# Strassen's seven half products in place of eight in a SwiGLU feed-forward on one Trainium2 core

## The chip, the core and the metric

The kernel runs on one core of one Trainium2 chip, in one launch. The metric is the device time of one execution in microseconds. Engines are named as in the profile: PE is TensorE (matmuls), PEld its weight loads, DVE the vector engine, ACT the scalar engine, POOL the GpSimd engine, SP the engine whose queue issues the DMAs. SBUF is the on-chip working memory, PSUM the eight banks of 512 fp32 columns into which matmuls accumulate.

## What is computed

One layer of a hybrid diffusion backbone on 128 context tokens and 512 latent tokens of width 1024: a modulated RMSNorm, one input projection, a bidirectional gated DeltaNet beside a Conformer branch, a gated merge and an output projection, and then the feed-forward, which alone the change touches. Cut to that (FF_DIM is 2816):

```python
h2 = rmsnorm(x, norm2) * (1 + sc2) + sh2
gu = h2 @ w_gu                                   # (640, 1024) @ (1024, 2 * 2816)
x = x + g2 * ((jax.nn.silu(gu[..., :FF_DIM]) * gu[..., FF_DIM:]) @ w_down)
y = rmsnorm(x, norm_f)
```

All inputs and outputs are fp32.

## The kernel before

The 640 tokens are five tiles of 128. Activations that feed a projection stand transposed: 128 channels on the partitions, tokens along the columns. Each fp32 operand of a large matmul is split into a high part (ACT copies it to the rounded type fp32r) and a low part (`split`, L106 to L108: the difference, on DVE or POOL), and each product is three matmuls: high x high, high x low, low x high, all accumulating in one bank.

The feed-forward goes by column tiles of 128 of the 2816 gate and up columns, 22 in all. For a tile, `load_w` (L117) loads two weight blocks (gate and up), each 1024 channels x 128 columns laid out as 8 k tiles, into one of four raw slots ("wr", cycled by `w_next`); the high part goes into one of two "wh" buffers, the low part takes the raw slot's place ("wl"; here POOL makes it). `proj` (L131) runs 8 k tiles x 3 terms x 2 column groups (256 and 384 tokens) for each of the two. ACT applies Silu to gate from PSUM (L1252), DVE multiplies by up from PSUM (L1254), and the product "ft" is split into "fh" and "fl".

The tiles go in three parts of 8, 8 and 6. After each part, `tok_proj` multiplies the part's tiles by their rows of w_down, for each of two halves of 512 output columns: the blocks of two k tiles go one after the other over the five token tiles, and the last `tail` blocks are left to a loop over token tiles that ends each tile's sum and calls `done`. There `residual` (L1129, L1130) multiplies the sum by the gate row and adds it to x1. In the last part `done` goes on with the sum of squares (L1134, L1137), a power on POOL (L153), the products with norm_f (L1204, L1209) and with the row scale (L1211 to L1215), and the output DMA. The last half of the last part keeps all of its three w_down blocks (`load_end`).

The first two tiles are run in two steps, first over the two token tiles that are ready (their 256-column group), while the norm of the others (`after_wo`, which writes h2h and h2l) is still under way. Engines work their queues in order. The order is made when the program is built: a list scheduler takes the instructions by priority (the order of the program, but for the scans of the DeltaNet, which come first) and by when their inputs and buffers are ready in its own timeline. Buffers of a tag ("wh", "sub", "C", "H") are given out when an instruction is scheduled; the "wr" slots and, after the change, "v2" and "F" are bound when the program is written.

Of the kernel before, what the change touches and what calls it, by code (L numbers as in the profile page):

```python
# [9 lines left out]
F32 = mybir.dt.float32  # L10
# [46 lines left out]
def hybrid_step(ctx, tc, I, O):  # L57
# [5 lines left out]
    base = -(-nc.sbuf_base // 32) * 32  # L63
    nc.alloc_sbuf_tensor("weights", [P, 1024 * NWR], F32)
    w_slots = [(nc.alloc_sbuf_tensor_at(f"wr{i}", [P, 1024], F32, offset=base + 4096 * i).ap(),
# [9 lines left out]

    BUFS = {"wh": NWH, "sub": 3, "H": 4, "K": 4, "Q": 3, "C": 4, "F": 2, "dd": 3, "v2": 3, "S": 1}
    SIZE = {"wh": 1024, "sub": 1024, "H": 4 * COLS, "K": CONV + 3 * COLS,
            "Q": 4 * COLS, "C": CONV + 4, "F": COLS, "dd": 256, "v2": 512, "S": 512}

    def T_(tag, name, dt=F32, cols=None):  # L80
        return sb.tile([P, cols or SIZE[tag]], dt, tag=tag, name=name, bufs=BUFS[tag])

# [17 lines left out]
    def g3(ap, a):  # L100
        return ap.rearrange("p (a b) -> p a b", a=a)
# [26 lines left out]
    def cols_of(w, c0, n=P):  # L128
        return w[:, c0:c0 + n].rearrange("(k p) c -> p k c", p=P)
# [937 lines left out]

    def s2_tile(name):
        return s2p.tile([P, 1024], F32R, tag="w2", name=name, bufs=6)

# [126 lines left out]
    def after_down(n, last):
        def done(i, pt):
# [19 lines left out]

    def load_end(src, lo_eng=None):
        wh = s2_tile("wh2")  # L1220
        wr, wl = next(w_next)
        nc.sync.dma_start(out=g3(wr, 2), in_=src)
        split(wh, wl, wr, V)
        return g3(wh, 2), g3(wl, 2)

    f0 = 0
    for part, nf in enumerate((8, 8, 6)):
        fh = [g3(T_("H", f"fh{q}", F32R), 4) for q in range(2)]
        fl = [g3(T_("H", f"fl{q}", F32R), 4) for q in range(2)]
        for f in range(nf):  # L1230
            if f0 + f == 0:

                cut, early2 = HALVES, []
                for k in range(2):
                    w2 = w_first if k == 0 else [load_w(cols_of(wgu, FF * j + 128), lo_eng=(V, G)[j],
                                                        wh=s2_tile("wh2")) for j in range(2)]
                    early2.append((w2, mm_pair()))
                    for w, pb in zip(*early2[k]):
                        proj(w, h2h, h2l, NK, (pb, None), (0,), cut, True)
            if f0 + f < 2:  # L1240
# [12 lines left out]
            for s, d in halves(pup, t, cut):
# [34 lines left out]
```

## Time and profile before

| | us |
|---|---|
| median of 3 runs | 1339.76 (1338.90 to 1341.18) |
| the profiled execution, its own time | 1341.02 |
| its span, first to last instruction | 1339.2 |

The profile is of one execution. Times in its rows are microseconds from the start of the span, except where a mean duration stands in nanoseconds. A matmul's duration includes its pipeline; the pace of a stretch is its length divided by its matmuls. An idle time is put down to the instruction that came last of those that were waited for.

### The profile page before, as it was taken

The page shows a single profiled execution, that of the slowest core. Times are in us where ns is not written, and L with a number is a line of the kernel's source. Part 1 is how long each engine was busy: PE and PEld are TensorE (multiplying, and loading weights), DVE is VectorE, ACT ScalarE, POOL GpSimd, SP SyncE. Part 2 cuts the span into 40 slices and gives each one's busy share as a digit, 9 for nine tenths or more (in the row PEclk, how much of TensorE's full clock was granted, in tenths as well). Part 3 has the DMA queues.
Part 4 walks back from the last instruction along what each step waited for, and adds up shares of the span by engine and source line. Part 5 has one row for each costly group of instructions (what it writes and reads, how often), then busy time and mean ns, then how long its engine had stood idle before and what let it go on. Part 6 is the DMA issues. An engine that isn't in the chain of part 4 may idle for free.

```text
span 1339.2 us, 23242 instructions
## 1 busy us (share of the span) xinstructions
PE 1278.0 (95%) x9180; PEld 1203.7 (90%) x9180; DVE 845.0 (63%) x1663; ACT 505.2 (38%) x1080; POOL 299.7 (22%) x306
## 2 busy tenths in 40 slices
PE   4998998997999999999998999999999999999997
PEld 4998997997998999999988998899988999889996
DVE  5788996989667899998687774621224212243136
ACT  3426646254354554525354323422221222112223
POOL 2103312220110312211010036433300333003304
PEclk8998999999999999999999999999999999999999
DMA  9523353343343453324456882122222222222222
GB/s 290 153 64 97 113 167 123 112 139 99 109 122 102 142 144 101 105 78 128 142 188 202 286 281 87 52 76 79 79 74 70 78 80 75 68 79 79 79 68 91
DMA packets 180333, 157.31 MB, mean 117 GB/s; under 512 B 9072, under 2 KB 151809, under 8 KB 180225
## 3 DMA queue, kind: packets, MB, share of 16 engines
q1 hardware_dynamic: 180225, 155.83, 37.6%
q8 instruction: 72, 1.18, 0.4%
q14 instruction: 36, 0.29, 0.1%
HBM read 131.80 MB, written 24.00 MB: 116 GB/s over the span
## 4 chain that ended last, share of the span: by engine, by line
PE 57%; DVE 8%; DMA 3%; issue 2%; ACT 2%; POOL 1%; SPq 0%; POOLq 0%; DVEq 0%; ACTq 0%
PE mm L143 36%; PE sm L1108 9%; PE mm L1108 4%; PE sm L143 1%; DVE wl L108 1%; PE sm L729 1%; DVE uacc L843 1%; PE sm L753 1%; PE sm L656 1%; DVE uacc L840 1%; PE sm L1153 1%; PE sm L716 1%; PE sm L709 1%; PE sm L739 1%; DMA wr<-in_w_in 1%
## 5 line engine op out<-in xcount | busy, mean ns | idle before, releaser
L107 ACT ACTIVATE wh<-wr 128x1024 fp32r<-128x1024 f32 (+1 forms) x154 | 152.6, 992 | 477.2 <-PE mm L143 186.1
L143 PE MATMUL mm<-hh,wh 128*128 128x256 f32 (+1 forms) x896 | 217.6, 318 | 0.9 <-ACT wh L107 0.9
L143 PE MATMUL mm<-hl,wh 128*128 128x256 f32 (+1 forms) x896 | 215.4, 314 | 0.0
L108 POOL TENSOR_TENSOR wl<-wr,wh 128x1024 fp32r<-128x1024 f32 (+1 forms) x59 | 133.2, 2259 | 356.7 <-ACT wh L107 337.2
L143 PE MATMUL mm<-hh,wl 128*128 128x256 f32 (+1 forms) x896 | 212.5, 314 | 0.0
L108 DVE TENSOR_TENSOR wl<-wr,wh 128x1024 fp32r<-128x1024 f32 (+1 forms) x95 | 109.7, 1155 | 105.7 <-ACT wh L107 94.4
L143 PEld LDWEIGHTS mm<-hh,wh 128*128 128x128 f32 x896 | 161.5, 190 | 6.8 <-issue 4.6
L143 PEld LDWEIGHTS mm<-hl,wh 128*128 128x128 f32 x896 | 164.5, 189 | 0.0
L143 PEld LDWEIGHTS mm<-hh,wl 128*128 128x128 f32 x896 | 162.7, 189 | 0.3 <-issue 0.2
L143 PE MATMUL mm<-h2h,wh 128*128 128x256 f32 (+1 forms) x672 | 155.7, 309 | 0.0
L143 PE MATMUL mm<-h2l,wh 128*128 128x256 f32 (+1 forms) x672 | 154.9, 308 | 0.0
L143 PE MATMUL mm<-h2h,wl 128*128 128x256 f32 (+1 forms) x672 | 154.6, 307 | 0.0
L1254 DVE TENSOR_TENSOR ft<-ft,mm 128x256 f32<-128x256 f32 (+1 forms) x42 | 18.6, 481 | 189.9 <-PE mm L143 189.8
L143 PEld LDWEIGHTS mm<-h2l,wh 128*128 128x128 f32 x672 | 123.1, 188 | 0.0
L143 PEld LDWEIGHTS mm<-h2h,wl 128*128 128x128 f32 x672 | 122.7, 188 | 0.0
L143 PEld LDWEIGHTS mm<-h2h,wh 128*128 128x128 f32 x672 | 122.0, 188 | 0.2
L478 DVE SCALAR_TENSOR_TENSOR acc<-ci,colA,acc 128x642 f32<-128x642 f32 x96 | 85.8, 894 | 7.6 <-ACT acc L476 7.1
L1108 PE MATMUL sm<-wh,fl 128*128 128x512 f32 x152 | 60.0, 395 | 0.0
L1108 PE MATMUL sm<-wh,fh 128*128 128x512 f32 x152 | 59.8, 393 | 0.0
L1108 PE MATMUL sm<-wl,fh 128*128 128x512 f32 x152 | 59.6, 392 | 0.0
L108 DVE TENSOR_TENSOR fl<-ft,fh 128x640 fp32r<-128x640 f32 x22 | 46.5, 2112 | 16.5 <-ACT fh L107 16.5
L604 DVE TENSOR_TENSOR stmp<-M,X 128x30 f32<-128x30 f32 (+14 forms) x120 | 44.6, 372 | 2.6 <-POOL X L598 1.0
(347 smaller groups left out, 2446.8 us busy)
## 6 DMA issues: line engine op xcount, KB each, us to landing
wr<-in_w_in SPq DMA_DIRECT2D x56, 512.0 KB
wr<-in_w_gu SPq DMA_DIRECT2D x44, 512.0 KB
wr<-in_w_ada SPq DMA_DIRECT2D x32, 512.0 KB
wr<-in_w_down SPq DMA_DIRECT2D x22, 512.0 KB
wada<-in_w_ada SPq DMA_DIRECT2D x8, 1024.0 KB
atd<-et SPq DMA_DIRECT2D x40, 128.0 KB
aux<-atd SPq DMA_DIRECT2D x40, 128.0 KB
tgd<-tgt SPq DMA_DIRECT2D x16, 320.0 KB
```

The source lines that it names most:

```text
L107: S_.activation(hi, x, AF.Identity)
L108: return (lo_eng or V).tensor_tensor(out=lo, in0=x, in1=hi.bitcast(F32), op=ALU.subtract)
L143: PE.matmul(out, a[:, kt, :], x, start=(kt == 0 and j == 0), stop=(kt == nk - 1 and j == 2))
L478: V.scalar_tensor_tensor(out=acc[:, :n], in0=ci[:, k:k + n], scalar=vA[:, k, ct:ct + 1], in1=acc[:, :n], op0=ALU.mult, op1=ALU.add)
L604: V.tensor_tensor(out=t, in0=bc(M[:, j + 1:, j:j + 1], [P, n, j]), in1=bc(X[:, j:j + 1, 0:j], [P, n, j]), op=ALU.mult)
L656: PE.matmul(pt[:, j, :], lhs[j], rhs[j], start=True, stop=True)
L709: PE.matmul(pr[:, d, j, :], TT[j].kT[:, ck[d], :], S[:, d, j, :], start=True, stop=True)
L716: PE.matmul(pq[:, d, j, :], TT[j].q2[:, OFFC[ck[d]]:OFFC[ck[d]] + P], S[:, d, j, :], start=True, stop=True)
L729: PE.matmul(pv[:, d, j, :], Y1[:, d, j, ck[d], :], rhs, start=True, stop=True)
L739: PE.matmul(pS[:, d, j, :], TT[j].ktok[:, ck[d], :], vw[:, d, j, :], start=True, stop=True)
L1108: PE.matmul(acc[i], a[kt // 4][:, kt % 4, c], b[:, k2, :], start=(kt == 0 and j == 0), stop=(kt == nk - 1 and j == 2))
L1254: V.tensor_tensor(out=d, in0=d, in1=s, op=ALU.mult)
```

## The change

For 19 of the 22 column tiles (all but the first three), gate and up, split into channel halves, form a 2 x 2 block matrix (a11, a12: gate, first and second 512 channels; a21, a22: up), and the transposed activations one of channel halves by token halves (b11 to b22, 64 of each token tile's 128 tokens: 320 columns). Eight half products become seven, in a variant of Strassen's scheme that shares its sums.

- `gate_up`, per tile: loads the same two blocks; DVE makes four sums of 512 columns; seven 512-column operands are split (ACT the high part, POOL the low); seven products of 4 k tiles x 3 terms with 320 columns; ACT copies the first from PSUM, DVE adds seven times from PSUM, ACT makes two Silus, DVE two products into ft, and ft is split as before.
- `sums`, once: four sums of activation blocks, each from high and low parts, and their splits: per k tile of a half ten DVE sums and four splits of 320 columns, with the low parts on DVE.
- The parts are 3, 4, 4, 4, 3 and 4 tiles, with one set of fh and fl of 4 tiles; down has 24 blocks in place of 22, and 60 residuals in place of 30.
- `load_end` goes; the last half has `tail` 2 of its 2 blocks and uses load_w.
- Buffers: "v2" (3 of 512 columns) and "F" (2 of 640) become fixed blocks, given out in turn; the four sums of a tile take four of these five. The seven high parts take four buffers out of the cycle wh, sub, sub, wh, sub, w2. The half products' banks are given out as sm, ma, sm, mb, which are all eight. norm_f's row moves to two other places, in two DMAs.

```diff
     base = -(-nc.sbuf_base // 32) * 32
-    nc.alloc_sbuf_tensor("weights", [P, 1024 * NWR], F32)
+
+    fixed = {"v2": (3, 512), "F": (2, COLS)}
+    nc.alloc_sbuf_tensor("weights", [P, 1024 * NWR + sum(n * c for n, c in fixed.values())], F32)
+    homes, at = {}, base + 4096 * NWR
+    for tag, (n, c) in fixed.items():
+        homes[tag] = []
+        for i in range(n):
+            homes[tag].append({dt: nc.alloc_sbuf_tensor_at(f"{tag}{i}{nm}", [P, c], dt, offset=at).ap()
+                               for dt, nm in ((F32, "f"), (F32R, "r"))})
+            at += 4 * c
+        homes[tag] = cycle(homes[tag])
...
-    BUFS = {"wh": NWH, "sub": 3, "H": 4, "K": 4, "Q": 3, "C": 4, "F": 2, "dd": 3, "v2": 3, "S": 1}
+    BUFS = {"wh": NWH, "sub": 3, "H": 4, "K": 4, "Q": 3, "C": 4, "dd": 3, "S": 1}
...
     def T_(tag, name, dt=F32, cols=None):
+        if tag in homes:
+            return next(homes[tag])[dt]
         return sb.tile([P, cols or SIZE[tag]], dt, tag=tag, name=name, bufs=BUFS[tag])
...
-    def s2_tile(name):
-        return s2p.tile([P, 1024], F32R, tag="w2", name=name, bufs=6)
+    def s2_tile(name, tag="w2", cols=1024):
+        return s2p.tile([P, cols], F32R, tag=tag, name=name, bufs=2 if tag == "T" else 1)
...
-        wh = s2_tile("wh2")
+        if q % 2 == 0:
+            whole.append(s2_tile("wh2", "T", 4 * COLS))
+        wh = whole[-1][:, 1024 * (q % 2):1024 * (q % 2) + 1024]
...
-            wr, wl = T_("sub", "wr2"), s2_tile("wl2")
+            wr, wl = T_("sub", "wr2"), T_("sub", "wl2", F32R) if q == 2 else s2_tile("wl2")
...
-    g2b = T_("Q", "g2b")[:, :2 * D].rearrange("p (r c) -> p r c", r=2)
+    g2t = T_("Q", "g2b")
+    g2b = g2t[:, :2 * D].rearrange("p (r c) -> p r c", r=2)
     for r in range(2):
         nc.sync.dma_start(out=g2b[:, r, :], in_=gdr[1, r].partition_broadcast(P))
-    nfb = T_("sub", "nfb")
-    nc.sync.dma_start(out=nfb, in_=I["norm_f"].partition_broadcast(P))
+    nfb = [g2t[:, 2 * D:], T_("S", "nfb")]
+    for n in range(2):
+        nc.sync.dma_start(out=nfb[n], in_=I["norm_f"][512 * n:512 * n + 512].partition_broadcast(P))
...
-    def load_end(src, lo_eng=None):
...
+    HT = 64
+    T4 = NCH * 4 * HT
+    fh = [g3(T_("H", "fh", F32R), 4)]
+    fl = [g3(T_("H", "fl", F32R), 4)]
+
+    def sums():
+
+        both = [T_("H", "tb", F32R) for _ in range(2)] + [s2_tile("tb", "T", 4 * COLS) for _ in range(2)]
+        hi = [t[:, :T4].rearrange("p (i k c) -> p i k c", k=4, c=HT) for t in both]
+        lo = [t[:, T4:2 * T4].rearrange("p (i k c) -> p i k c", k=4, c=HT) for t in both]
+        for k in range(4):
+            ta, tb = T_("C", "t12")[:, :COLS], T_("C", "t34")[:, :COLS]
+            f = [g3(t[:, c:c + NCH * HT], NCH) for t in (ta, tb) for c in (0, NCH * HT)]
+            (b11, b12), (b21, b22) = ([[t[:, :, k, HT * b:HT * b + HT].bitcast(F32) for t in (h2h[q], h2l[q])]
+                                       for b in range(2)] for q in range(2))
+
+            def op(n, a, b, o):
+                V.tensor_tensor(out=f[n], in0=a, in1=b, op=o)
+            op(0, b12[0], b11[0], ALU.subtract)
+            op(0, f[0], b12[1], ALU.add)
+            op(0, f[0], b11[1], ALU.subtract)
+            op(1, b22[0], f[0], ALU.subtract)
+            op(1, f[1], b22[1], ALU.add)
+            op(2, b22[0], b12[0], ALU.subtract)
+            op(2, f[2], b22[1], ALU.add)
+            op(2, f[2], b12[1], ALU.subtract)
+            op(3, b21[0], f[1], ALU.subtract)
+            op(3, f[3], b21[1], ALU.add)
+            for n in range(4):
+                split(hi[n][:, :, k], lo[n][:, :, k], f[n])
+        return list(zip(hi, lo))
+
+    hi_tag, sum_tag = cycle(("wh", "sub", "sub", "wh", "sub", "w2")), cycle(("v2", "F", "v2", "F", "v2"))
+    bank_tag = cycle(("sm", "ma", "sm", "mb"))
+
+    def gate_up(f, k):
+        raw = []
+        for j in range(2):
+            wr, wl = next(w_next)
+            nc.sync.dma_start(out=g3(wr, NK), in_=cols_of(wgu, FF * j + 128 * f))
+            raw += [(wr[:, c:c + 512], wl[:, c:c + 512]) for c in (0, 512)]
+        a11, a12, a21, a22 = raw
+        sm = []
+        for _ in range(4):
+            home = next(homes[next(sum_tag)])
+            sm.append((home[F32][:, :512], home[F32R][:, :512]))
+        for k_, (a, b, o) in enumerate(((a21, a22, ALU.add), (None, a11, ALU.subtract), (a11, a21, ALU.subtract),
+                                        (a12, None, ALU.subtract))):
+            x = (a or sm[0])[0]
+            y = (b or sm[1])[0]
+            V.tensor_tensor(out=sm[k_][0], in0=x, in1=y, op=o)
+        ops = []
+        for n, (x, lo) in enumerate((a11, sm[1], a12, sm[2], sm[0], a22, sm[3])):
+            if n % 2 == 0:
+                tag = next(hi_tag)
+                hi2 = s2_tile("wh") if tag == "w2" else T_(tag, "wh", F32R)
+            hi = hi2[:, 512 * (n % 2):512 * (n % 2) + 512]
+            split(hi, lo, x, G)
+            ops.append((g3(hi, 4), g3(lo, 4)))
+        b11, b21, b22 = ((h2h[q][:, :, :, HT * b:HT * b + HT], h2l[q][:, :, :, HT * b:HT * b + HT])
+                         for q, b in ((0, 0), (1, 0), (1, 1)))
+        t1, t2, t3, t4 = tsum
+        right = (b11, t2, b21, t3, t1, t4, b22)
+
+        def product(n):
+            (wh, wl), (xh, xl) = ops[n], right[n]
+            tag = next(bank_tag)
+            bank = ps.tile([P, 512], F32, tag=tag, name="mm", bufs=4 if tag == "sm" else 2)[:, :NCH * HT]
+            for kt in range(4):
+                for j, (a, b) in enumerate(((wh, xh), (wh, xl), (wl, xh))):
+                    PE.matmul(g3(bank, NCH), a[:, kt, :], b[:, :, kt, :], start=(kt == 0 and j == 0),
+                              stop=(kt == 3 and j == 2))
+            return bank
+
+        def add(out, a, pt):
+            V.tensor_tensor(out=out, in0=a, in1=pt, op=ALU.add)
+        N2 = NCH * HT
+        ca, cb = T_("C", "ca"), T_("C", "cb")
+        c11, c12, c21, c22 = ca[:, :N2], ca[:, N2:2 * N2], cb[:, :N2], cb[:, N2:2 * N2]
+        t = T_("C", "ft")[:, :COLS]
+        tv = t.rearrange("p (i c) -> p i c", c=2 * HT)
+        S_.activation(c11, product(0), AF.Identity)
+        add(c12, c11, product(1))
+        add(c11, c11, product(2))
+        S_.activation(c11, c11, AF.Silu)
+        add(c21, c12, product(3))
+        p5 = product(4)
+        add(c22, c21, p5)
+        add(c12, c12, p5)
+        add(c21, c21, product(5))
+        V.tensor_tensor(out=tv[:, :, :HT], in0=g3(c11, NCH), in1=g3(c21, NCH), op=ALU.mult)
+        add(c12, c12, product(6))
+        S_.activation(c12, c12, AF.Silu)
+        V.tensor_tensor(out=tv[:, :, HT:], in0=g3(c12, NCH), in1=g3(c22, NCH), op=ALU.mult)
+        split(fh[0][:, k, :], fl[0][:, k, :], t)
+    early2 = []
+
+    for k in range(2):
...
-    for part, nf in enumerate((8, 8, 6)):
...
+    PARTS = (3, 4, 4, 4, 3, 4)
+    for part, nf in enumerate(PARTS):
+        for k in range(nf):
+            f = f0 + k
+            if part:
+                gate_up(f, k)
+                continue
...
+            if f == 1:
+                tsum = sums()
...
-            split(fh[f // 4][:, f % 4, :], fl[f // 4][:, f % 4, :], t)
+            split(fh[0][:, k, :], fl[0][:, k, :], t)
+        last = part == len(PARTS) - 1
         for n in range(2):
-            end = part == 2 and n == 1
-            tok_proj(wd, 128 * f0, nf, n, fh, fl, after_down(n, part == 2), 3 if end else 1, V,
-                     load=load_end if end else None)
+            tok_proj(wd, 128 * f0, nf, n, fh, fl, after_down(n, last), 2 if last and n else 1, V)
```

## Rows read from the trace of the kernel before

**Rows 1.** The page: busy time of two engines with their share, and in 40 slices the busy tenths of PE and POOL and the granted clock of PE.
```profile
PE 1278.0 (95%) x9180; PEld 1203.7 (90%) x9180; DVE 845.0 (63%) x1663; ACT 505.2 (38%) x1080; POOL 299.7 (22%) x306
...
PE   4998998997999999999998999999999999999997
...
POOL 2103312220110312211010036433300333003304
PEclk8998999999999999999999999999999999999999
```

**Rows 2.** The chain of waits in order of time: start us, us, what. The first is a stretch of the trunk, whose moving operand is contiguous; the others are the feed-forward.
```profile
497.98 19.86 PE mm L143 x135
...
866.38 7.48 PE mm L143 x63
...
879.57 16.85 PE sm L143 x96
896.42 84.81 PE mm L143 x576
981.23 5.54 PE sm L1108 x24
...
995.09 5.55 PE sm L1108 x24
...
1036.69 113.06 PE mm L143 x768
...
1302.49 1.17 PE mm L1108 x5
```

**Rows 3.** Groups by line and shape, 800 us to the end, of DVE, POOL and ACT: line, engine, operation, output and inputs, shapes, count, busy us, mean ns, idle before.
```profile
L1130 DVE TENSOR_TENSOR x<-x,tr 128x512 f32<-128x512 f32 x40 | 39.4, 998 | 0.9
...
L108 DVE TENSOR_TENSOR wl<-wr,wh 128x1024 fp32r<-128x1024 f32 x23 | 28.2, 1225 | 73.5 <-ACT wh L107 62.6 <-issue 10.6
L1129 DVE TENSOR_TENSOR tr<-sm,g2b 128x512 f32<-128x512 f32 x20 | 13.5, 685 | 15.0 <-PE sm L1108 15.0
L1254 DVE TENSOR_TENSOR ft<-ft,mm 128x384 f32<-128x384 f32 x20 | 10.9, 547 | 0.0
...
L1254 DVE TENSOR_TENSOR ft<-ft,mm 128x256 f32<-128x256 f32 x22 | 9.3, 421 | 189.9 <-PE mm L143 189.8
...
L108 POOL TENSOR_TENSOR wl<-wr,wh 128x1024 fp32r<-128x1024 f32 x51 | 122.2, 2398 | 327.0 <-ACT wh L107 327.0
...
L107 ACT ACTIVATE wh<-wr 128x1024 fp32r<-128x1024 f32 x74 | 78.3, 1060 | 339.9 <-issue 106.8 <-PE mm L143 106.8 <-PE mm L1108 95.5
L107 ACT ACTIVATE fh<-ft 128x640 fp32r<-128x640 f32 x22 | 16.3, 740 | 3.5 <-DVE ft L1254 3.5
...
L1252 ACT ACTIVATE ft<-mm 128x384 f32<-128x384 f32 x20 | 9.7, 483 | 0.0
L1252 ACT ACTIVATE ft<-mm 128x256 f32<-128x256 f32 x22 | 8.0, 365 | 0.0
L107 ACT ACTIVATE h2h<-hf 128x512 fp32r<-128x512 f32 x10 | 6.3, 630 | 0.3
```

**Rows 4.** Busy us (and instructions) of PE, PEld, DVE, ACT and POOL, granted clock, DMA share and GB/s in the gate/up stretch of the second part.
```profile
1036.00:1150.00 114.00, 114.00 (x774) 113.83 (x773) 29.28 (x28) 27.79 (x40) 35.93 (x15) 1.00 0.25 75
```

**Rows 5.** Timelines of DVE and POOL: start us, us, engine, line, operation. First the free durations (a residual's addition and fl, nothing on POOL), then DVE beside POOL, in three places.
```profile
897.89 0.83 DVE L108 TENSOR_TENSOR fl<-ft,fh 128x640 fp32r<-128x640 f32 x1 [0.81 <-ACT fh L107]
...
1034.56 0.69 DVE L1130 TENSOR_TENSOR x<-x,tr 128x512 f32<-128x512 f32 x1
...
911.50 2.38 POOL L108 TENSOR_TENSOR wl<-wr,wh 128x1024 fp32r<-128x1024 f32 x1 [4.67 <-ACT wh L107]
912.20 2.38 DVE L108 TENSOR_TENSOR fl<-ft,fh 128x640 fp32r<-128x640 f32 x1 [0.81 <-ACT fh L107]
...
1030.99 2.39 POOL L108 TENSOR_TENSOR wl<-wr,wh 128x1024 fp32r<-128x1024 f32 x1 [60.57 <-ACT wh L107]
1031.18 0.69 DVE L1129 TENSOR_TENSOR tr<-sm,g2b 128x512 f32<-128x512 f32 x1 [6.00 <-PE sm L1108]
1031.91 2.02 DVE L1130 TENSOR_TENSOR x<-x,tr 128x512 f32<-128x512 f32 x1
...
848.73 2.54 POOL L108 TENSOR_TENSOR h2l<-hf,h2h 128x512 fp32r<-128x512 f32 x2 [2.74 <-ACT h2h L107]
...
867.15 1.61 DVE L1130 TENSOR_TENSOR x<-x,tr 128x512 f32<-128x512 f32 x1
868.14 4.33 POOL L108 TENSOR_TENSOR h2l<-hf,h2h 128x512 fp32r<-128x512 f32 x3
```

**Rows 6.** Timelines of POOL and ACT where the first tiles run: the last writes of h2l, and the order of ACT in tile 2.
```profile
877.16 2.58 POOL L108 TENSOR_TENSOR h2l<-hf,h2h 128x512 fp32r<-128x512 f32 x2 [2.00 <-ACT h2h L107]
...
903.29 1.06 ACT L107 ACTIVATE wh<-wr 128x1024 fp32r<-128x1024 f32 x1 [5.43 <-PE mm L143]
904.26 0.74 ACT L1252 ACTIVATE ft<-mm 128x256 f32<-128x256 f32 x2
```

**Rows 7.** The end, as DVE's timeline (the residual of each of the last token tiles), and a group of the trunk's scan.
```profile
1324.04 0.68 DVE L1129 TENSOR_TENSOR tr<-mm,g2b 128x512 f32<-128x512 f32 x1
...
1328.16 0.68 DVE L1129 TENSOR_TENSOR tr<-mm,g2b 128x512 f32<-128x512 f32 x1
...
1331.65 0.69 DVE L1129 TENSOR_TENSOR tr<-mm,g2b 128x512 f32<-128x512 f32 x1 [0.43 <-PE mm L1108]
...
1334.93 0.49 DVE L1215 TENSOR_SCALAR yo<-yo,s 128x512 f32<-128x512 f32 x1 [0.66 <-POOL s L153]
...
L739 PE MATMUL sm<-vw,K 128*128 128x128 f32 x128 | 18.5, 282 | 4.2 <-DVE vw L735 4.2
```

More of the change, by code (lines that the diff above doesn't have):

```diff
@@ L74, in hybrid_step @@
     ps = es(tc.tile_pool(name="ps", bufs=4, space=PSUM))
-    BUFS = {"wh": NWH, "sub": 3, "H": 4, "K": 4, "Q": 3, "C": 4, "F": 2, "dd": 3, "v2": 3, "S": 1}
-    SIZE = {"wh": 1024, "sub": 1024, "H": 4 * COLS, "K": CONV + 3 * COLS,
-            "Q": 4 * COLS, "C": CONV + 4, "F": COLS, "dd": 256, "v2": 512, "S": 512}
+    BUFS = {"wh": NWH, "sub": 3, "H": 4, "K": 4, "Q": 3, "C": 4, "dd": 3, "S": 1}
+    SIZE = {"wh": 1024, "sub": 1024, "H": 4 * COLS, "K": CONV + 3 * COLS, "Q": 4 * COLS, "C": CONV + 4, "dd": 256, "S": 512}
     def T_(tag, name, dt=F32, cols=None):
+        if tag in homes:
+            return next(homes[tag])[dt]
         return sb.tile([P, cols or SIZE[tag]], dt, tag=tag, name=name, bufs=BUFS[tag])
@@ L1184, in load_whole @@
         return g3(wh, 2), g3(wl, 2)
-    kept = []
+    kept, whole = [], []
     tok_proj(wo, 0, NK, 0, mh, ml, after_wo(0), 2)
     tok_proj(wo, 0, NK, 1, mh, ml, after_wo(1), 4, ahead=load_first, load=load_whole)
-    g2b = T_("Q", "g2b")[:, :2 * D].rearrange("p (r c) -> p r c", r=2)
+    g2t = T_("Q", "g2b")
+    g2b = g2t[:, :2 * D].rearrange("p (r c) -> p r c", r=2)
     for r in range(2):
         nc.sync.dma_start(out=g2b[:, r, :], in_=gdr[1, r].partition_broadcast(P))
-    nfb = T_("sub", "nfb")
-    nc.sync.dma_start(out=nfb, in_=I["norm_f"].partition_broadcast(P))
+    nfb = [g2t[:, 2 * D:], T_("S", "nfb")]
+    for n in range(2):
+        nc.sync.dma_start(out=nfb[n], in_=I["norm_f"][512 * n:512 * n + 512].partition_broadcast(P))
     def after_down(n, last):
@@ L1203, in done @@
             if n == 0:
-                G.tensor_tensor(out=xv, in0=xv, in1=nfb[:, :512], op=ALU.mult)
+                G.tensor_tensor(out=xv, in0=xv, in1=nfb[0], op=ALU.mult)
             else:
@@ L1208, in done @@
                 c = slice(512, D)
-                (G if i < 4 else V).tensor_tensor(out=y[:, c], in0=x1[1][:, i, :], in1=nfb[:, c], op=ALU.mult)
+                (G if i < 4 else V).tensor_tensor(out=y[:, c], in0=x1[1][:, i, :], in1=nfb[1], op=ALU.mult)
                 si = s1[:, i:i + 1]
@@ L1217, in after_down @@
         return done
-    def load_end(src, lo_eng=None):
[L1220 to L1224, printed above, removed]
-    f0 = 0
-    for part, nf in enumerate((8, 8, 6)):
[L1228 to L1240, printed above, removed]
+    HT = 64
@@ new lines, in hybrid_step @@
+    early2 = []
+    for k in range(2):
+        w2 = w_first if k == 0 else [load_w(cols_of(wgu, FF * j + 128), lo_eng=(V, G)[j],
+                                            wh=T_("sub", "wh2", F32R) if j else s2_tile("wh2")) for j in range(2)]
+        early2.append((w2, mm_pair()))
+        for w, pb in zip(*early2[k]):
+            proj(w, h2h, h2l, NK, (pb, None), (0,), HALVES, True)
+    f0 = 0
+    PARTS = (3, 4, 4, 4, 3, 4)
[5 more added lines that the diff above has]
+                continue
+            if f < 2:
@@ L1241, in hybrid_step @@
                 pgt, pup = [(pb, sm_ps()) for pb in early2[f][1]]
                 for w, pp in zip(early2[f][0], (pgt, pup)):
-                    proj(w, h2h, h2l, NK, pp, (1,), cut, True)
+                    proj(w, h2h, h2l, NK, pp, (1,), HALVES, True)
             else:
-                cut = HALVES
-                w2 = [load_w(cols_of(wgu, FF * j + 128 * (f0 + f))) for j in range(2)]
+                w2 = [load_w(cols_of(wgu, FF * j + 128 * f)) for j in range(2)]
                 pgt, pup = [mm_pair() for _ in range(2)]
@@ L1248, in hybrid_step @@
                 for w, pp in zip(w2, (pgt, pup)):
-                    proj(w, h2h, h2l, NK, pp, (0, 1), cut, True)
+                    proj(w, h2h, h2l, NK, pp, (0, 1), HALVES, True)
+            if f == 1:
+                tsum = sums()
             t = T_("C", "ft")[:, :COLS]
-            for s, d in halves(pgt, t, cut):
+            for s, d in halves(pgt, t):
                 S_.activation(d, s, AF.Silu)
-            for s, d in halves(pup, t, cut):
+            for s, d in halves(pup, t):
```

## The prediction, made before the changed kernel was run

> **What bounds the kernel now.** I read the engines' shares first, to find the full engine: TensorE is busy 95% of the span, and in the slices the feed-forward (from about 866 us on) shows 9 in every slice at full granted clock [rows 1]. Then the chain of waits in order of time: from 866 us to 1303 us it is matmuls without a break, at L143 (gate/up) and L1108 (down) [rows 2]. Nothing else sets the pace there, so a removed matmul is worth its pitch, as long as what feeds the rest keeps up. The pitch is read from the same rows: 576 matmuls in 84.81 us, 0.1472 us each, alternating 256 and 384 columns. The stretch with 256 columns alone gives 7.48/63 = 0.119, the one with 384 alone 16.85/96 = 0.1755; a 512-column one takes 5.55/24 = 0.231 [rows 2]. Time goes with columns, so 320 columns should cost the mean of the first two, 0.147. Third, the groups by shape and the stage table: in the gate/up stretch of 1036 to 1150 us (eight tiles) DVE is busy 29 us, ACT 28 and POOL 36 of 114 [rows 3, 4]. They look idle enough. Fourth, the timelines of DVE and POOL side by side, since the change gives both more: there the cover is thinner than the shares say [rows 5].
>
> **The change, part by part.**
>
> *Matmuls.* A gate/up tile has 2 matrices x 8 k tiles x 3 terms x 2 column groups = 96 matmuls; the new one 7 products x 4 k tiles x 3 terms = 84, of 320 columns. 96 x 0.1472 = 14.13 us, 84 x 0.1472 = 12.37; 1.77 saved, and x19 tiles is **-33.6 us**. The moving operand is now read in runs of 64 columns where it was 128. No row has that. The contiguous operand of the trunk has the same pitch as the 128-column runs (19.86/135 = 0.147 [rows 2]), so I cost the runs at nothing; the other end is the pitch of 384 columns, 0.1755, at which a tile takes 14.74. The 660 down matmuls are the same.
>
> By the Trainium skill, "TensorE: Matmul & The Clock Gate", section Back-to-back issue gap, an isolated warm matmul takes N/2.4 + 2.5 ns, an estimate of 136 ns for 320 columns; the gain would be 31.0 us. The rows here are slower than that for every width, and I use the rows.
>
> *Weight splits.* Each tile had two 1024-column splits (ACT high part 1.06, POOL low part 2.40 us [rows 3]); now seven of 512. ACT: 7 x 0.63 (the h2h row) + three passes over 320 columns at about 0.42 (between the 365 and 483 ns forms) + 0.74 for fh = 6.4 us of 12.4. POOL: two in a row took 2.54 us, so 7 x 1.27 = 8.9 us [rows 3, 5].
>
> *DVE.* Per tile four 512-column sums (0.69 each, the free duration in rows 5), two 320-column products (0.49, on the line through 0.69 and 0.82), fl (0.82), and seven adds from PSUM (0.49, between the 421 and 547 ns forms [rows 3]): 2.8 + 1.0 + 0.8 + 3.4 = 8.0 us. That alone fits under 12.4.
>
> *DVE against POOL.* A DVE operation with both inputs in SBUF does not run beside a POOL one: L1130 started at 1031.91 while POOL's split ran to 1033.38, and ended 0.55 us after that, at 1033.93; free, it takes 0.69. fl ended 0.70 after its POOL neighbour. L1129, which reads PSUM, took 0.69 beside the same POOL split. And three POOL splits with one DVE operation let in took 4.33 instead of 3.81 [rows 5]. So these two lists share one resource: 8.9 + 4 x 0.55 + 2 x 0.35 + 0.70 = 12.5 us per tile, against 12.37 for TensorE. Before it was 2 x 2.4 + 0.7 of 14.1. This is the cover of all that I cost at nothing, and it is gone: equal loads with nothing to spare.
>
> *What is late next.* The sums' blocks: five of them ("v2" three, "F" two), four used per tile, so the second operand of tile f+1 (sm[1]) takes the block that product 4 of tile f frees. From there to its use TensorE has products 5, 6 and the next 0: 3 x 1.77 = 5.3 us. The path: two adds queued ahead on DVE 1.0, the sum 0.69 with half a POOL split of waiting 0.6, ACT 0.63, POOL 1.27 with about 0.5 of waiting: 4.7. With full waits (1.27 twice) it is 6.1. So it is just in time, or 0.8 us late. Behind that sum, DVE holds the next adds (eight PSUM banks cover these), and ACT's Silu holds the next high parts. The first tile of each of the five parts is prepared under the down stage (120 x 0.231 = 27.7 us), which leaves 14 tiles exposed. Lower bound 0, upper bound the second rival below; nearest to the mid path, with a full port, I take 0.6 us each: **+8.4 us**.
>
> *sums().* 56 DVE operations of 320 columns x 0.49 = 27.4 us, once. They can start when the last h2l is written (877.16 + 2.58 = 879.7 [rows 6]). The part after needs them far later, but they stand ahead of tile 1's own products in the program, and tile 2's up matmuls need the banks that those free, at 896.42 + 7.07 = 903.5. 879.7 + 27.4 + 1.4 (tile 0's DVE work) + 1.0 = 909.5: 6 us late if all of the sums go first, 8.4 if one POOL split is waited for too, none if tile 1's go between. I take **+4**.
>
> *Six parts for three.* 30 more residuals (0.69 + 0.69 [rows 3, 5]) on DVE: 41 us, under 20 to 28 us of matmuls per down stage, where ten take 13.8 and four low parts of w_down 4 x 1.23 = 4.9 [rows 3]. Hidden, 0; were it not, the excess would show in the banks, which the next stage needs only after 6.9 us.
>
> *The end.* The last down half has 12 matmuls per token tile, 2.77 us, where it had 18, 4.16. The chain behind them (residual, sum of squares, power, output) runs at 4.12 us per token tile [rows 7], so far level with TensorE, which is last waited for at 1331.65. If the order of DVE stays as it is, 2.77 + 4 x 4.12 - 13.9 = 5.4 us come back; if the next residual goes ahead, nothing. load_end with its own buffers is gone: the second w_down block waits for the "wh" of the stage before, 1.06 + 1.23 less 1.39 of cover, 0.9 us, or 2.3 behind one residual. Bounds 0 and 7.7; **+2.5**.
>
> *Moved homes.* "v2" and "F" are now bound to a block when written, not when scheduled; the scan of the trunk uses them. The idle time that the trunk's scan matmuls spend on vw, 4.2 us [rows 7], may double or go: 0, bounds -4 and +4. norm_f's two DMAs are as many bytes and are due 450 us later: 0.
>
> **Sum.** 1341.0 (the profiled execution) - 33.6 + 8.4 + 4 + 2.5 = 1322.3. It lies 1.3 above the median of the runs, so **1321** as a median.
>
> **Rivals.**
> *Clean:* everything stays hidden. For it speaks that the loads only tie and the first tile of a part is ahead; against it the tie itself. 1341.0 - 33.6 - 1.3 = 1306.
> *The shared resource is held for whole durations.* Then a tile needs 8.9 + 4 x 0.69 + 2 x 0.49 + 0.82 = 13.45 us there, 1.08 over TensorE: 19 x 1.08 = 20.5 in place of the 8.4, 1333. Against it: 0.55 of 0.69 and 0.70 of 0.82 showed [rows 5]. The Trainium skill, "SBUF — State Buffer", section Who interferes with whom, states this form: the pair is an exclusive lock, held for the whole instruction, and the second to issue fully blocks. That one blocks, the rows agree; that the start-up counts, they don't.
>
> *DVE loses to POOL (slower):* seven two-SBUF operations per tile each wait for POOL. DVE's tile is 3.4 + 4.6 + 7w; with w = 1.27 (every one meets a fresh split) 16.9 us, 2.7 above the old tile: 1340 + 19 x 2.7 = 1391. It decides against the change at 14.13, w = 0.88. Against it: POOL has only seven splits per tile, and free waiting would be 0.72 x 0.64 = 0.46 on average, 11.2 us.
> *The queue order (slower):* sm[1]'s sum is issued behind the last products of the tile before. Then the path starts at that tile's end: add 0.49, Silu 0.42, product 0.49, then 0.69 + 0.63 + 1.27 and one POOL wait 1.27 = 5.3 us against 1.77 of cover: 3.5 us x 14 = 49, in place of the 8.4: 1321 - 8.4 + 49 = 1362. It decides at 2.4 us per tile. Against it: the order before puts the next tile's splits ahead of this one's Silu (903.29 before 904.26 [rows 6]).
> *The half products don't run at 320 columns' price:* at 0.1755 a tile is 0.6 us longer than before, with room again for the splits: 1340 + 11.6 + 6.5 (sums and end) = 1358. Break-even is 0.168. For it speaks only that no row has such runs; against it, that contiguous and 128-column operands cost the same [rows 2].
>
> **How the numbers follow.** Clean 0.20 (1306, with the trunk's 4 us down to 1302); the forecast 0.43 (own range 1309 to 1335: clean plus 3, and the forecast plus double stalls and the end's full price); whole durations 0.12 (1333); the remainder that eats the gain to within 0.2% (2.7 us, about what a measurement here can tell) 0.05; DVE against POOL 0.09, the queue order 0.08, the price of half products 0.03. Faster 0.75, same 0.05, slower 0.20. The range runs from 1302 over the first four cases and a little into the slower ones, to 1345.
>
> **What would show it.** Right: a pitch of 0.147 us in the new matmuls, 12.4 us per tile inside a part plus gaps of about half a microsecond at the second product, DVE's sums and fl stretched beside POOL, and one gap near 903 us. Wrong: gaps at every product (DVE or POOL as the pace), a gap after each tile's end (queue order), a pitch above 0.15, or a tail longer than 7.5 us after the last matmul.

## The result and the profile after

The changed kernel took 1325.14 us (median; 1320.71 to 1325.81) against 1339.33 for the kernel before beside it (1338.51 to 1341.18). The ratio is 0.9885, with a 95% interval of 0.9861 to 0.9909: 14.2 us faster, 4 us more than the forecast time. The profiled execution of after took 1324.89 us, span 1323.0.

The page of after, as in [rows 1]: the shares of two engines, and the slices of PE, POOL and the granted clock.

```profile
PE 1246.2 (94%) x8952; PEld 1164.8 (88%) x8952; DVE 1042.3 (79%) x1990; ACT 561.3 (42%) x1212; POOL 413.7 (31%) x401
...
PE   4998998997999999999999999998999999999996
...
POOL 2103312220001311221010026340664726463755
PEclk8999998999999999999999999999999999999998
```

DVE went from 63% to 79% and POOL from 22% to 31%, in the feed-forward from mostly 3 and less to mostly 4 to 7 tenths. PE shows 9 there, but for an 8 in the 28th slice (893 to 926 us), a 6 at the end where [rows 1] has 7, and the granted clock of the last slice at 8. The chain of waits of after, answering to [rows 2], from the end of a down stage through a part of four tiles into the next down stage (start us, us, what):

```profile
1093.00 1.40 PE mm L1119 x6
1094.40 35.23 PE mm L1306 x241
1129.62 0.02 issue
1129.65 0.04 DVE ca L1311
1129.68 0.37 issue
1130.05 0.48 DVE cb L1311
1130.53 0.40 DVE ca L1311
1130.93 1.24 DVE v20f L1286
1132.17 0.02 issue
1132.19 0.64 ACT wh L118
1132.83 0.04 issue
1132.87 11.97 PE mm L1306 x80
1144.85 5.59 PE sm L1119 x24
```

In the kernel before, 768 gate/up matmuls stood in one piece [rows 2]. Here the half products at L1306 run at 35.23/241 = 0.146 us each, as cheap as hoped, and then the chain leaves TensorE: it goes over two adds of DVE, a sum of weights "v20f" that takes 1.31 us (1.24 in the chain) instead of 0.69 [rows 5], and ACT's high part of it. These 336 matmuls took 50.45 us, 1094.40 to 1144.85; without a gap they take 49.20 (an experiment below). Why the sum was late is seen in the timelines of DVE and POOL (start us, us, engine, line, operation):

```profile
1130.45 0.48 DVE L1311 TENSOR_TENSOR ca<-ca,mm 128x320 f32<-128x320 f32 x1
1130.85 1.31 DVE L1286 TENSOR_TENSOR v20f<-v22f,wr 128x512 f32<-128x512 f32 x1
...
1130.31 1.29 POOL L119 TENSOR_TENSOR F1r<-F1f,wh 128x512 fp32r<-128x512 f32 x1
```

POOL's split ended at 1131.60 and DVE's sum 0.56 us after it, the picture of [rows 5], now inside a tile. The operations by shape, DVE's of after in the second to sixth part (936 to 1282 us; count, busy us, mean ns, idle before), answer to [rows 3]:

```profile
L1141 DVE TENSOR_TENSOR x<-x,tr 128x512 f32<-128x512 f32 x45 | 42.4, 961 | 0.5
L1311 DVE TENSOR_TENSOR ca<-ca,mm 128x320 f32<-128x320 f32 x75 | 35.7, 480 | 9.0 <-PE mm L1306 8.8
...
L1329 DVE TENSOR_TENSOR ft<-ca,cb 128x320 f32<-128x320 f32 x18 | 21.3, 1182 | 3.4 <-ACT ca L1328 3.4
L119 DVE TENSOR_TENSOR fl<-ft,fh 128x640 fp32r<-128x640 f32 x18 | 19.3, 1074 | 12.9 <-ACT fh L118 12.9
...
L1326 DVE TENSOR_TENSOR ft<-ca,cb 128x320 f32<-128x320 f32 x18 | 17.8, 991 | 1.2
```

The adds that read PSUM (L1311) take 480 ns, as costed. Everything here with two SBUF inputs is stretched: the products to 991 and 1182 ns where 490 was costed, fl to 1074 from 820. POOL's splits of 512 columns are stretched too, to 1550 ns from 1270:

```profile
L119 POOL TENSOR_TENSOR wl<-wr,wh 128x512 fp32r<-128x512 f32 x57 | 88.3, 1550 | 55.7 <-ACT wh L118 24.1 <-DVE v20f L1286 8.4 <-DVE v22f L1286 6.3
```

### The profile page after: what moved, and what is told of

Read it like the earlier page. It is cut to its first block, busy times and chain, and to the rows that moved or that the text cites. A ratio compares the mean times of both kernels' runs of the same rounds, so it can differ in the third digit from the quotient of the medians.

```text
span 1323.0 us, 23525 instructions
## 1 busy us (share of the span) xinstructions
PE 1246.2 (94%) x8952; PEld 1164.8 (88%) x8952; DVE 1042.3 (79%) x1990; ACT 561.3 (42%) x1212; POOL 413.7 (31%) x401
## 5 line engine op out<-in xcount | busy, mean ns | idle before, releaser
L119 POOL TENSOR_TENSOR wl<-wr,wh 128x512 fp32r<-128x512 f32 (+1 forms) x78 | 130.4, 1675 | 119.2 <-ACT wh L118 75.3
L119 DVE TENSOR_TENSOR wl<-wr,wh 128x1024 fp32r<-128x1024 f32 (+1 forms) x97 | 115.8, 1194 | 61.2 <-ACT wh L118 60.4
L1306 PE MATMUL mm<-tb,wh 128*128 128x320 f32 x608 | 132.7, 308 | 2.8 <-ACT wh L118 2.6
L1306 PEld LDWEIGHTS mm<-tb,wh 128*128 128x128 f32 x608 | 100.8, 188 | 4.0 <-ACT wh L118 3.4
L1306 PE MATMUL mm<-h2l,wh 128*128 128x320 f32 x228 | 70.7, 310 | 0.0
L1306 PE MATMUL mm<-h2h,wh 128*128 128x320 f32 x228 | 70.5, 309 | 0.0
L1141 DVE TENSOR_TENSOR x<-x,tr 128x512 f32<-128x512 f32 x70 | 65.5, 953 | 0.8
L1119 PE MATMUL sm<-wh,fh 128*128 128x512 f32 x160 | 62.0, 397 | 3.2 <-ACT wh L118 3.2
L1119 PE MATMUL sm<-wl,fh 128*128 128x512 f32 x160 | 63.1, 394 | 0.0
L1119 PE MATMUL sm<-wh,fl 128*128 128x512 f32 x160 | 61.4, 391 | 0.0
L1306 PE MATMUL mm<-h2h,wl 128*128 128x320 f32 x152 | 47.4, 312 | 1.9 <-POOL wl L119 1.9
L527 POOL TENSOR_TENSOR rn<-rn,mhalf 128x5 f32<-128x5 f32 x16 | 21.5, 1347 | 84.6 <-DVE rn L526 84.6
L1311 DVE TENSOR_TENSOR ca<-ca,mm 128x320 f32<-128x320 f32 x76 | 36.2, 480 | 9.1 <-PE mm L1306 8.8
```

What stands on the lines that cost most here:

```text
L527: G.tensor_tensor(out=rn[:, j], in0=rn[:, j], in1=bc(mhalf, [P, NCH]), op=ALU.pow)
L1119: PE.matmul(acc[i], a[kt // 4][:, kt % 4, c], b[:, k2, :], start=(kt == 0 and j == 0), stop=(kt == nk - 1 and j == 2))
L1141: V.tensor_tensor(out=xv, in0=xv, in1=t, op=ALU.add)
L1306: PE.matmul(g3(bank, NCH), a[:, kt, :], b[:, :, kt, :], start=(kt == 0 and j == 0), stop=(kt == 3 and j == 2))
L1311: V.tensor_tensor(out=out, in0=a, in1=pt, op=ALU.add)
```

## The experiments

The theory under test: the saved matmuls are worth what the pitch says; four prices are paid for them, namely the resource that DVE and POOL share, the place of sums() ahead of tile 1, the tail, and the finer parts (nothing). Each edit below is against the changed kernel. Gaps inside the tiles are read as the stretch from the first to the last half product of a part, less 0.231 us for each down matmul that stands in it, against the same stretch of a kernel without gaps (49.04 us for four tiles, 36.75 for three).

**no_pool: POOL's low parts left out; the third term takes the high part again.**

```
-            split(hi, lo, x, G)
-            ops.append((g3(hi, 4), g3(lo, 4)))
+            S_.activation(hi, x, AF.Identity)
+            ops.append((g3(hi, 4), g3(hi, 4)))
```

> The low parts of the 19 tiles' gate/up operands are left out: POOL makes none, and the third term of each half product uses the high part again, so TensorE, ACT and DVE do the same work. My theory (DVE's operations with two SBUF inputs wait for POOL's splits, and this is what holds TensorE up between tiles): the sums take 0.69 us each again in place of 1.0 to 1.8, fl 0.82, and the 7 us of gaps inside the 19 tiles go: 1318. Rival (the gaps come from the few blocks for the sums, or from loads): the DVE operations get shorter, but at least 5 us of gaps remain, 1323 to 1325.

Measured: 1315.61, ratio 0.9823 [0.9803, 0.9842], 9.5 us less than the change. Its chain of waits for the same part, and its groups, as above:

```profile
1088.36 1.40 PE mm L1119 x6
1089.76 49.20 PE mm L1306 x336
1138.96 5.59 PE sm L1119 x24
```

```profile
L1311 DVE TENSOR_TENSOR ca<-ca,mm 128x320 f32<-128x320 f32 x75 | 36.3, 484 | 17.6 <-PE mm L1306 16.8 <-ACT fh L118 0.8
L1141 DVE TENSOR_TENSOR x<-x,tr 128x512 f32<-128x512 f32 x45 | 30.0, 686 | 0.4
...
L119 DVE TENSOR_TENSOR fl<-ft,fh 128x640 fp32r<-128x640 f32 x18 | 14.8, 825 | 13.4 <-ACT fh L118 13.4
...
L1329 DVE TENSOR_TENSOR ft<-ca,cb 128x320 f32<-128x320 f32 x18 | 8.8, 491 | 10.9 <-ACT ca L1328 10.9
```

Four tiles are one piece of 49.20 us: 0.1464 us per matmul, 12.30 per tile. With POOL silent the products go from 1182 to 491 ns and fl from 1074 to 825, while the adds from PSUM stay (480 and 484). So of the operations in a tile, those with two SBUF inputs share the resource, and the adds with one do not. The Trainium skill, "SBUF — State Buffer", section Who interferes with whom, says the same of a DVE instruction with two SBUF inputs and of one with at most one, outside the modes that use two ports; the trace agrees, with these numbers. The parts of after take 52.46, 50.81, 50.30, 36.78 (three tiles) and 51.92 us; here they take about 49.0 and 36.8. Three down matmuls stand in the first stretch of after, 0.7 us. The gaps of after are therefore 2.7 + 1.8 + 1.3 + 0 + 2.9 = 8.7 us, and they are nearly the whole gain of this run. The run takes away the sharing and the work in POOL's queue at once. That the sharing has a part in the gaps is seen in the stretched operations; how much of them is POOL's own slowness, no run here separates.

**low2_dve: two of the seven low parts on DVE.**

```
-            split(hi, lo, x, G)
+            split(hi, lo, x, V if n in (5, 6) else G)
```

> In the 19 tiles the low parts of operands 5 and 6 are made on DVE instead of POOL. By my theory the resource that DVE and POOL share is the tight one: per tile it holds 12.5 us now and 5 x 1.27 + 6 x 0.55 + 0.7 + 0.7 = 11.1 then, so the 7 us of gaps fall to 2 or less: 1319 to 1321. Rival (DVE's own queue is the tight one, by its order or its length: 8.0 us of work plus waits, now 9.4): gaps grow, 1328 or more.

Measured: 1320.75, ratio 0.985 [0.9827, 0.9873]. The parts take 50.75, 48.97, 49.33, 36.72 and 50.59 us: about 3.4 us of gaps in place of 8.7. The time fell by 4.4 us, which the two intervals alone do not tell from nothing. DVE got two more operations per tile, and TensorE waited less.

**pool_plus: an eighth subtraction of 512 columns on POOL per tile, which nobody reads.**

```
+            if n == 6:
+                S_.activation(hi, x, AF.Identity)
+                G.tensor_tensor(out=hi2[:, 512:], in0=x, in1=hi.bitcast(F32), op=ALU.subtract)
+                G.tensor_tensor(out=lo, in0=x, in1=hi.bitcast(F32), op=ALU.subtract)
+            else:
+                split(hi, lo, x, G)
```

> One more POOL subtraction of 512 columns per tile, into a half of a buffer that nobody reads (1.27 us each, 19 in all). My theory (the shared resource is full, 12.5 us per tile against 12.4 of TensorE): 13.8 us per tile, so each of the 14 tiles that are not prepared under a down stage gives up to 1.3 us more: 1335 to 1343. Rival (there is slack of a tile or more, and the gaps come from elsewhere): within 2 us of 1325.

Measured: 1332.74, ratio 0.9945 [0.9924, 0.9966]: 7.6 us more than the change. The parts take 56.57, 51.16, 50.55, 36.79 and 54.47, with 11 down matmuls in the first and two in the last: 13.6 us of gaps, 4.9 more. The sign is the theory's and the rival (within 2 us) falls, but the size is short of the 10 to 18 us expected: 1.27 us more per tile cost 0.4 per tile in time and 0.26 in gaps. So the resource was not full all the time; lulls took in two thirds or more.

**blocks6: a sixth block for the sums of a tile** (half of norm_f's row, which had it, moves elsewhere). The prediction had named one place, sm[1] waiting for the block that product 4 of the tile before frees.

```
-    fixed = {"v2": (3, 512), "F": (2, COLS)}
+    fixed = {"v2": (3, 512), "F": (2, COLS), "S": (1, 512)}
...
-    hi_tag, sum_tag = cycle(("wh", "sub", "sub", "wh", "sub", "w2")), cycle(("v2", "F", "v2", "F", "v2"))
+    hi_tag, sum_tag = cycle(("wh", "sub", "sub", "wh", "sub", "w2")), cycle(("v2", "F", "v2", "F", "v2", "S"))
```

> Six blocks for the sums in place of five (the block of S joins, norm_f's second half moves elsewhere), so that a tile's second operand no longer waits for product 4 of the tile before. If the few blocks make the gaps, the gaps inside the 19 tiles (9.3 us over the pace of the stretch without POOL) fall to 3 or less: 1319. If they come from DVE and POOL sharing, as I hold, POOL and DVE have the same work in the same time and most of the gaps stay: 1322 to 1326.

Measured: 1324.87, ratio 0.9886 [0.9861, 0.9911], no difference. The parts take 52.45, 48.95, 50.21, 36.66 and 51.83, with no down matmul in the first: 7.2 us of gaps, 1.5 less. The block is at most a fifth of the gaps.

**sums_late: sums() behind tile 1's own products in the program.**

```
-            if f == 1:
-                tsum = sums()
             t = T_("C", "ft")[:, :COLS]
...
             split(fh[0][:, k, :], fl[0][:, k, :], t)
+            if f == 1:
+                tsum = sums()
```

> The call of sums() stands behind tile 1's own products instead of ahead of them; nothing else differs. My theory (the sums go first on DVE and hold tile 1's products until 909.6 us, so that TensorE stands still at 902 to 907 us): TensorE's idle time there, 3.4 + 0.3 + 0.6 + 0.3 = 4.6 us, goes, tile 1's products run before 900 us, and the median falls from 1325 to about 1320.5. Rival (the wait is for something else that the early stage needs, such as weights or banks): the gap stays, 1325.

Measured: 1318.42, ratio 0.9842 [0.9821, 0.9863]: 6.7 us less than the change, though the two intervals just overlap. First TensorE and DVE of after around the gap, then DVE of sums_late at tile 1's product; then, of both kernels, the busy us (and counts) of PE, PEld, DVE, ACT and POOL, granted clock, DMA share and GB/s, after first:

```profile
906.00 1.17 PE L1119 MATMUL sm<-wh,fh 128*128 128x512 f32 x2 [3.21 <-ACT wh L118]
907.38 0.58 PE L154 MATMUL mm<-h2h,wh 128*128 128x256 f32 x1 [0.22 <-ACT ft L1361]
...
908.19 0.41 PE L154 MATMUL mm<-h2h,wh 128*128 128x256 f32 x1
908.40 0.41 PE L154 MATMUL mm<-h2l,wh 128*128 128x256 f32 x1
```

```profile
909.58 0.41 DVE L1363 TENSOR_TENSOR ft<-ft,mm 128x256 f32<-128x256 f32 x1
909.91 0.54 DVE L1363 TENSOR_TENSOR ft<-ft,sm 128x384 f32<-128x384 f32 x1
```

```profile
899.63 0.55 DVE L1361 TENSOR_TENSOR ft<-ft,sm 128x384 f32<-128x384 f32 x1
```

```profile
905.00:908.00 3.00, 1.78 (x5) 1.07 (x6) 3.00 (x8) 2.41 (x6) 0.00 (x0) 0.68 0.28 110
908.00:911.00 3.00, 3.00 (x21) 3.00 (x21) 3.00 (x7) 1.78 (x5) 0.00 (x0) 0.75 0.02 5
```

```profile
905.00:908.00 3.00, 3.00 (x23) 3.00 (x22) 3.00 (x7) 2.35 (x6) 0.00 (x0) 1.00 0.00 0
```

In after, tile 1's two products are at 909.58 and 909.91; in sums_late the second of them is at 899.63, TensorE has 23 matmuls in 905 to 908 us where after has 5, and there is no gap. So the place is the one predicted. The releasers differ a little: what TensorE waited for was ACT, whose high part of a w_down block and whose Silu of tile 1 stood behind the high parts of the sums, each waiting for DVE. And behind the gap the granted clock had fallen to 0.68 and 0.75: matmuls of 256 columns start 0.21 us apart (908.19, 908.40) where they took 0.119 [rows 2].

**six_parts: the full products of before in all 22 tiles, with the changed parts, end and buffers.**

```
-            if part:
-                gate_up(f, k)
-                continue
...
-            if f == 1:
-                tsum = sums()
```

> The structure of the change without its half products: six parts of 3 to 4 tiles, 60 residuals, one fh and fl, the new end, the moved blocks, but all 22 tiles by full products and no sums(). My theory (thirty more residuals are hidden under the down stages; the end costs 1.3 us of waiting for the last w_down block and 4 us of a longer tail): 1339.5 + 5 = 1343 to 1346. Rival (residuals and part changes cost TensorE time, some 1 us at each of the three added changes, or the moved blocks slow the trunk): 1348 or more. Other rival (the structure is free): 1339 to 1341.

Measured: 1346.34, ratio 1.0057 [1.0038, 1.0075], 7 us slower than the kernel before. TensorE's waits from 860 us on (line, releaser: us in total, times, longest):

```profile
PE sm L1164 <- DVE dg L1160: 1.0, 1, 1.0
PE mm L1119 <- DVE tr L1140: 0.7, 1, 0.7
```

So the frame of the change costs 7 us by itself, and the half products with their sums bring 1346.3 - 1325.1 = 21 us. Between the parts the residuals show nowhere, as predicted. What shows is a wait in the last half (L1119) for a residual of the half before (tr, L1140), a wait near 871 us, at the end of the trunk, for an operation of DVE (dg, L1160), and a tail that is 3 us longer.

**The versions built on these.** If POOL's part is a cost, DVE alone should do better, until DVE is full. All four have sums_late's edit; late_dve2 adds that of low2_dve, late_alldve gives all seven low parts to DVE, and the two with "_end" also move POOL's products with norm_f in the last half to DVE.

```
-            split(hi, lo, x, G)
+            split(hi, lo, x, V)
...
-                (G if i < 4 else V).tensor_tensor(out=y[:, c], in0=x1[1][:, i, :], in1=nfb[1], op=ALU.mult)
+                V.tensor_tensor(out=y[:, c], in0=x1[1][:, i, :], in1=nfb[1], op=ALU.mult)
```

> sums() behind tile 1's products and the low parts of operands 5 and 6 on DVE, together. The two gains are at different places, so they should add: 6.7 and 4.4 us from 1325 give 1314. If one is only the other seen twice (a state of the whole queue), 1317 to 1319.

> sums() behind tile 1's products, and all seven low parts of a tile on DVE, none on POOL. Nothing is shared any more, but DVE has 8.0 + 7 x 0.69 = 12.8 us per tile against 12.3 of TensorE. If sharing was the whole trouble and DVE's own length counts as it stands, DVE is the pace: the 9.3 us of gaps of the stage go, and 0.5 us in each of the 14 exposed tiles come: 1318.4 - 9.3 + 7 = 1316. If DVE's order (a queue in which products, sums and low parts wait for one another) costs more than its length: 1325 or more.

> The same, and in the last half the products with norm_f of all token tiles on DVE, none on POOL. My theory of the tail (11.5 us after the last matmul instead of 7.6, because POOL's products hold up the power and the residual's additions behind them): the tail falls by 1 to 2 us, 1312.5. Rival (DVE itself is the pace there, 14.3 us of work for five token tiles against 13.9 of matmuls): the same as without, or longer.

> late_alldve, and the last products with norm_f on DVE for all token tiles. The tail after the last matmul (10.9 us there) should fall to about 9.3, as it did with the same edit on late_dve2: 1309. Rival: the tail's gain is lost in DVE's length again, 1310.7.

Measured: late_dve2 1313.13 (0.981 [0.9788, 0.9831]), late_alldve 1310.71 (0.9791 [0.9774, 0.9808]), late_dve2_end 1312.73 (0.9804 [0.9784, 0.9825]), late_alldve_end 1311.76 (0.9811 [0.9787, 0.9834]). late_alldve was expected at 1316, slower than late_dve2; that it is slower is not borne out. It lies 7.7 us below sums_late, from which it differs in the low parts alone. Its median is also 2.4 us below late_dve2's, but these two intervals overlap; in the traces the gaps inside the tiles are 3.2 us in late_dve2 and 1.3 in late_alldve. Its chain and its DVE:

```profile
1009.51 49.21 PE mm L1306 x336
...
1086.71 49.29 PE mm L1306 x336
```

```profile
1041.03 0.69 DVE L1286 TENSOR_TENSOR v20f<-wr,wr 128x512 f32<-128x512 f32 x1
1041.63 0.48 DVE L1311 TENSOR_TENSOR cb<-ca,mm 128x320 f32<-128x320 f32 x1
1042.03 0.69 DVE L119 TENSOR_TENSOR wl<-wr,wh 128x512 fp32r<-128x512 f32 x1
1042.63 0.68 DVE L119 TENSOR_TENSOR v20r<-v20f,wh 128x512 fp32r<-128x512 f32 x1
1043.24 0.48 DVE L1311 TENSOR_TENSOR ca<-ca,mm 128x320 f32<-128x320 f32 x1
```

These parts are one piece again, 49.2 us; the last part alone keeps 1.3 us of gaps. A 512-column operation lasts 0.69 us, but the next one starts 0.60 us after it; a 320-column one 0.48 and 0.40. By starts a tile's own work on DVE is 4 x 0.60 + 9 x 0.40 + 0.73 = 6.7 us, and seven low parts add 4.2: 10.9, under the 12.3 of TensorE. The stage from 936 to 1270 us shows the trade, after first and late_alldve second (columns as above):

```profile
936.00:1270.00 334.00, 328.65 (x1966) 306.26 (x1965) 260.07 (x351) 125.26 (x212) 191.84 (x127) 1.00 0.27 81
```

```profile
936.00:1270.00 334.00, 333.21 (x2010) 312.43 (x2009) 276.99 (x487) 128.46 (x216) 0.00 (x0) 1.00 0.27 83
```

DVE does 136 operations more for 17 us more of busy time, while TensorE does 44 matmuls more: the others no longer wait for POOL within theirs. The Trainium skill, "GPSIMD Engine Reference", section Engine selection, gives elementwise work to VectorE and puts GPSIMD at about half its speed for two inputs; the trace agrees (1.27 against 0.60 to 0.69 us), and adds that the slower engine also held up the faster one.

**best2, and late_dve2 once more.** best2 is late_dve2_end with own buffers for the w_down blocks of the last half, as `load_end` of before had them.

> As late_dve2_end, and the w_down blocks of the last half get their high parts in free 'sub' buffers (as load_end had its own before), so that the second block need not wait for the 'wh' of the half before. My theory: the 1.2 us of idle TensorE at 1287 us go, 1311.5. Rival (the end is set by DVE's tail whatever TensorE does): as without, 1312.7.

Measured: 1315.03 (0.9818 [0.9801, 0.9835]); late_dve2 again gave 1313.36 (0.9807 [0.9787, 0.9828]). TensorE's waits in the last half fell from 1.2 to 0.8 us, and the time did not fall. The intervals of all these versions overlap, so that the "_end" edits and best2 are not told from no change. late_alldve lies below sums_late, and those two intervals do not overlap; it is the fastest median of all, 14.4 us below the change and, by its ratio, 2.1% below the kernel before.

## Why the prediction was right, by its steps

**Matmuls: right.** Predicted -33.6 us. Without gaps a tile takes 12.30 us (no_pool), 14.13 - 12.30 = 1.83 less than before: -34.8. The runs of 64 columns cost nothing, and the rival of the half products' price is out.

**DVE against POOL: right in kind, and by some luck in size.** Predicted +8.4, measured 8.7 of gaps; but the 8.4 was 14 times 0.6 us at one place, and the gaps lie elsewhere (next step). POOL silent gives 9.5 us back, two low parts moved 4.4, one more costs 7.6. In the sum that waited, DVE ended 0.56 us after POOL's split (0.55 in the prediction), so the rival of whole durations, with 20.5 us, is out. The slower rivals, DVE against POOL and the queue order, decide from 1.8 and 2.4 us a tile; the 14 tiles behind a part's first have 8.7/14 = 0.6. (The 2.4 sets the saved matmuls alone against the queue order; with the sum's 6.5 us for sums and end it is 1.9. And [rows 1] shows 7, not 9, in the last slice. Neither changes the outcome.)

**What is late next: too narrow.** The step put each gap at sm[1] behind a freed block, in every tile alike. blocks6 took that wait away and left most of the gaps. They lie in the second and fourth tile of a part, at different products, none in first tiles (that was predicted), and the part of three tiles has none. The two parts that follow the short down stages have most, 2.7 and 2.9 us; that a shorter down stage lets less be prepared ahead fits this and was not tried by itself. Waits for ACT's high parts (2.6 us) and POOL's low parts (2.8 us) both end gaps, so no one queue does. Also not settled is why pool_plus cost only 0.3 to 0.4 us of each 1.27. One reason can be read: DVE's load of 8.0 us per tile was summed from durations, and by starts it is 6.7.

**sums(): right place, size missed.** Tile 1's product was predicted at 909.5 if all the sums go first, and its first half came at 909.58. I had taken +4 as the middle of 0 and 8.4. The order of the program was kept: 4.6 us of gaps in the trace, and 6.7 us in time by sums_late. About 1 us of the rest is the clock, ten matmuls at 0.21 for 0.119, so that the trace shows 5.6 of the 6.7. That term the prediction lacked.

**The end: nearer the upper bound.** +2.5 was taken of 0 to 7.7; it is 5.3: 1.3 us of wait, and a tail of 11.5 us after the last matmul in place of 7.6. The wait has the size that was given to the second w_down block (0.9 to 2.3), and that is luck. It stands before a matmul of the first block, and the trace ends it with a residual of the half before:

```profile
1298.93 0.50 PE L1119 MATMUL mm<-wh,fh 128*128 128x512 f32 x1 [1.05 <-DVE tr L1140]
```

By the order of the program that residual frees the bank; it stood on DVE behind two additions that took 2.67 us beside POOL's products. DVE kept its order in the tail, as the 5.4 us side of that step said. Part of the tail is the shared resource once more, as DVE and POOL of after show it. Two sums of one column lie beside POOL's products (0.14 us where POOL is still). Two products with the row scale (L1230), the second beside POOL, take 2.04 us where one alone takes 0.48. Each has one SBUF tensor and a column of scales as inputs, so two tensors are not the only way into the resource:

```profile
1305.15 1.27 DVE L1148 TENSOR_TENSOR s<-ss 128x1 f32<-128x1 f32 x1
...
1306.53 1.15 DVE L1148 TENSOR_TENSOR s<-ss 128x1 f32<-128x1 f32 x1
...
1308.93 2.04 DVE L1230 TENSOR_SCALAR yo<-yo,s 128x512 f32<-128x512 f32 x2
...
1304.64 3.02 POOL L1224 TENSOR_TENSOR yo<-x,nfb 128x512 f32<-128x512 f32 x2
```

Moving those products shortened the tail in the trace, but no time that could be measured came of it.

**The frame.** Between the parts of six_parts the residuals cost nothing, as said; in the last half one held up a bank. The wait near 871 us, some 1.5 us, was not seen coming. The trunk reached the first half tile at 863.7 us instead of 866.2; other runs of the same code lie from 862.3 to 868.4, so the moved homes show no effect.

**The sum now.** All terms as the traces show them: -34.8 + 8.7 + 5.6 + 5.3 + 1.5 - 2.5 = -16.2, the 16.2 us between the spans of the two profiled executions (1339.2 and 1323.0); the medians lie 14.2 apart. The forecast had -18.7: matmuls 1.2 better, 2.5 from the trunk, which is chance, and costs of 21.1 in place of 14.9, each a little above what I chose and within its bounds, but for the 871 us wait and the clock.

## What to carry to other kernels

Where two engines share a resource, add up their holds on it in a stage, not their busy shares: by these, DVE and POOL looked idle here [rows 4], and their holds, as summed, tied with TensorE. Before an engine that looks idle is given work, compare the time it holds the resource with that of the engine it relieves (1.27 against 0.60 us here); the helper can cost more than it carries. A bulk of preparation is best put in the program behind the small operations that the pacing engine needs next, even when it is itself not due for long: moving one call gave 6.7 us, of which the trace shows 5.6.

## What I had not expected of the hardware

TensorE stood from 902.5 to 906.0 us, and the granted clock was then 0.68 and 0.75 over two stretches of 3 us, with 256-column matmuls 0.21 us apart until about 909.5, the lower of its two levels (1.2 of 2.4 GHz); then they were 0.12 apart again. The gaps inside the tiles, up to 1.4 us each, left it at 1.00. In pool_plus one wait inside a tile was 2.5 us (951.4 to 953.9 us), and the lower level came there too: half products stood 0.27 us apart for ten matmuls, at a granted clock of 0.52 (columns as above).

```profile
955.00:957.00 2.00, 2.00 (x10) 2.00 (x9) 2.00 (x3) 1.07 (x3) 2.00 (x3) 0.52 0.00 0
```

And DVE's operations overlap by 0.08 to 0.09 us when they stand back to back, so that their durations overstate a full queue by 15 to 20%.
